# Eight modulation sums, four low parts and the order at the turn in a one-core decoder layer

## The chip, the cores and the metric

The kernel runs on one core of a Trainium2 chip. The core has a matrix engine (TensorE, called PE in the profile, with its weight loads as PEld), VectorE (DVE), ScalarE (ACT), GpSimd (POOL) and SyncE (SP), which only issues transfers; ACT and POOL issue transfers as well. Each engine runs its own list of instructions in order and waits for the others by semaphores. The metric is device time in microseconds (us), the median over several executions; less is better. The profile is of one further execution.

## The reference

One decoder layer over 512 positions of 1024 channels, in float32. A condition vector `c` gives six modulation vectors of 1024 numbers each, and the layer is a mixer followed by a gated convolution block:

```python
cond = jax.nn.silu(c)
mod = cond @ ada_w[l] + ada_b[l]
sh1, sc1, g1, sh2, sc2, g2 = jnp.split(mod[:, None, :], N_MOD, axis=-1)
...                                   # mixer: mLSTM heads and a convolution group
x = x + g1 * rms_norm(mix, mix_post_g[l])
u = rms_norm(x, ffn_pre_g[l]) * (1.0 + sc2) + sh2
up = causal_dwconv(u @ ffn_up[l], ffn_conv_w[l], ffn_conv_b[l])   # 3 taps
a, gt = jnp.split(up, 2, axis=-1)
f = (jax.nn.silu(gt) * a) @ ffn_down[l]                           # 2816 -> 1024
x = x + g2 * rms_norm(f, ffn_post_g[l])
```

The last modulation vector, `g2`, is used only in the last line, after the down projection.

## The kernel before

**Precision.** Every large product is made of three matmuls: each operand is split into a high part, which ACT rounds into a tile `...h`, and a low part `...l`, the operand minus its high part; high times high, low times high and high times low are added up in PSUM (`mm3`, L188 to L190, and L1093, L1459). So each tile of 128x512 weights costs ACT one instruction and somebody one subtraction. There are two ways for the subtraction. `split` (L1011 to L1015) and `w_split` (L169 to L172) let VectorE or GpSimd subtract. `added_split` (L1081 to L1087) has ACT write the negated operand into the low tile (L1085), and a GpSimd transfer that accumulates (L1086) adds the operand onto its rounded negative.

**Modulation.** The 6144 modulation numbers are 48 columns of 128. Each column is one sum: a 128x1024 row block of the transposed weights is loaded into a tile of the pool `adas` (two buffers of 512 KB each) and VectorE multiplies it with the condition and sums over the row (L155 in `ada_block`, L1149 in `ada_add`; the profile names the output `junk`). Columns 40 to 47 belong to `g2`. After them come `ada_done(40, 48)`, which adds the bias, and `gain(3, ...)`, both small.

**The up projection.** 22 units, each of 256 columns (128 of `a`, 128 of the gate), go in two ways. Units 0 to 7 are plain (`plain_unit`): the loop over m = 0 to 3 takes two units a turn, each of 48 matmuls of 128x512 (units 0 to 2 are begun in halves while the mixer ends). Each unit's result stands in two PSUM banks; ACT and VectorE apply the three taps (`conv3`, L995 and L997; `fa5c` is the `a` half of unit 5, `fg5c` its gate half), and `unit_out` (L1140) writes the product into a tile `F`. For i = 3 and 4 `token_forms` makes sums of the inputs on GpSimd (L1059) and VectorE.

Units 8 to 21 go in seven stages, m = 4 to 10. A stage takes one unit by a Strassen-like scheme (products p1, p7, p5, p6 first, L1093, into banks `upx`, `upz`, `upw`; then four VectorE sums in `between`, L1111 to L1114; then p2, p3, p4) and one plain unit, whose two halves stand between and behind. In a stage PE's order is: first products of the even unit, first half of the plain unit, last products of the even unit, second half of the plain unit. The forms of the next unit's weights (L1299, L1314, L1345, L1346, L1361) are VectorE subtractions of loaded blocks, followed by ACT and GpSimd splits. In stages 4 to 7 two modulation columns a stage are fetched and summed (`ada_fetch`, `ada_add`).

**The down projection.** 11 groups of weights, m = 0 to 10, in two passes. In the first pass VectorE makes three sums of the loaded blocks of a group (`forms1`, L1190 to L1192), four operands are split (`b_m` is the plain block, `t_m` the three sums), and PE makes the products p1, p5, p7 and p6, of six matmuls each for two token halves' banks. `part_b` gives the plain block's low part to the accumulating transfer; without it `parts1` has VectorE subtract it. In the kernel before, groups 0 to 5, 8, 9 and 10 have `part_b`. For groups 9 and 10 PE takes p1 of both, p5 of both, p6 of both, p7 of both: the *turn*. There VectorE adds the product sums to each other (`su`, L1439, then L1441, L1445, L1447), and the second pass adds p2, p3 and p4 (L1459) onto the same banks, with its own loads (`load2`), one VectorE sum (L1254) and three splits a group (`forms2`). `b_0` to `b_10` and `t_0` to `t_10` are names of both passes.

**What sets the order.** The lists of PE and SP are as written in the program. VectorE, ACT and GpSimd keep the written order inside three `in_order()` blocks (the end of the mixer with the first up halves; the stages 4 to 10 together with the first pass of the down projection and the turn; the last outputs). Elsewhere, as in the plain units and in the loop of the second pass, a scheduler that simulates the engines orders them by priorities and dependencies. A transfer that ACT issues stands in ACT's list, and the work behind it waits until its buffer is free.

Of the kernel before, what the change touches and what calls it, by code (L numbers as in the profile page):

```python
# [52 lines left out]
def decoder_layer(ctx, tc, w_glu0, x, xT, c, adaT, vecs, w_glu, w_qko, w_v0, w_v, w_out, w_up, w_down, out):  # L53
# [890 lines left out]
    with in_order():  # L944
        for tt in range(3):
            mix_last(tt, 0, 2 * KT - KA)
        up_split(1, raw1, slots, "t")
        r = chain_sums(0)
        up_split(1, raw1, slots, "t")
        r = chain_x(0, r)  # L950
        chain_u(0, r)
        turn_tile(0)
        mix_last(3, 0, 7)
        r = chain_sums(1)
        up_split(1, raw1, slots, "t")
        r = chain_x(1, r)
        chain_u(1, r)
        turn_out(0)
        turn_tile(1)
        mix_last(3, 7, 2 * KT - KA)  # L960
        r = chain_sums(2)
        turn_out(1)
        r = chain_x(2, r)
        up_split(1, raw1, slots, "t")
        chain_u(2, r)
        up_half(0, 0)
        turn_tile(2)
        r = chain_sums(3)
        up_split(2, raw2, wpool, "w")
        r = chain_x(3, r)  # L970
        up_split(2, raw2, wpool, "w")
        chain_u(3, r)
        up_half(0, 1)
        up_split(2, raw2, wpool, "w")
        early.append([cvbank(f"up2_{half}") for half in range(2)])
        up_half(0, 2, 0)
        turn_tile(3)
        turn_out(2)
        up_split(2, raw2, wpool, "w")
        turn_out(3)  # L980
    up_half(0, 2, 1)
# [156 lines left out]
    def unit_out(i, a, g, F):  # L1138
        S.activation(g, g, AF.Silu)
        V.tensor_tensor(out=F[:, (i % 2) * T : (i % 2 + 1) * T], in0=a, in1=g, op=ALU.mult)  # L1140

    def ada_fetch(i):
        r = adas.tile([P, D], F32, tag="ada", name=f"ada_{i}")
        nc.scalar.dma_start(r, adaT[i // 2][:, (i % 2) * D : (i % 2 + 1) * D])
        return r

    def ada_add(i, r):
        junk = small.tile([P, D], BF16, tag="junk", bufs=1, name=f"junk_{i}")
        V.scalar_tensor_tensor(out=junk, in0=r, scalar=1.0, in1=cb, op0=ALU.mult, op1=ALU.mult, accum_out=mod[:, i : i + 1])  # L1149
# [100 lines left out]
    def forms2(m, a=0, b=3):  # L1250

        r = loaded[m]
        if b == 3:
            behind_turn(V.tensor_tensor(out=r[2], in0=r[0], in1=r[2], op=ALU.subtract))  # L1254
        return parts(r, [(f"b2_{m}", 0), (f"b4_{m}", 1), (f"t4_{m}", 2)][a:b])
# [8 lines left out]
    for m in range(MS):  # L1264
        open_F(m)
        for i in (2 * m, 2 * m + 1):
            pa, pg = plain_unit(i)
            if m < MS - 1:
                unit_out(i, conv3(pa, i, f"fa{i}"), conv3(pg, NF + i, f"fg{i}"), Fs[m])
            elif i % 2 == 0:  # L1270
                even = pa, pg
# [18 lines left out]
    with in_order():  # L1290
# [14 lines left out]
        for m in range(MS, NM):  # L1305
# [50 lines left out]
            if more_to_come:  # L1356
# [3 lines left out]
                ada = [(n, ada_fetch(n)) for n in range(40 + 2 * (m - MS), 42 + 2 * (m - MS))] if m < MS + 4 else []  # L1360
# [13 lines left out]
            for n, r in ada:  # L1374
                ada_add(n, r)
            if m == MS + 4:
                ada_done(40, 48)
                gain(3, 40, "ffn_post_g")
# [19 lines left out]
        for m in range(3, NM):  # L1398
            forms1(m)
            if m < 6 or NM - G2A <= m < NM - 1:  # L1400
                part_b(m)
            parts1(m)
            if m == NM - 2:
                part_b(NM - 1)
# [18 lines left out]
        w2 = {}  # L1423
        for which in ("p1", "p5", "p6", "p7"):
            for m in range(M1, NM):
                prod1(m, which)
            if which == "p1":
# [3 lines left out]
                w2[0] = forms2(0)  # L1431
            elif which == "p5":
                sp5 = [slot(f"sp5_{q}") for q in range(2)]
                for q in range(2):
                    S.activation(sp5[q], p5[q], AF.Copy)
            elif which == "p6":
# [5 lines left out]
                w2[1] = forms2(1, 0, 1)  # L1442
            else:
# [4 lines left out]
                w2[1] |= forms2(1, 1, 3)  # L1448
# [17 lines left out]
    for m in range(NM):  # L1466
# [3 lines left out]
        if m > 1:  # L1470
            w2[m] = forms2(m)
# [140 lines left out]
```

## Time and profile before

| | |
|---|---|
| median of 3 runs | 780.53 us (780.48 to 781.32) |
| the profiled execution | 779.45 us |
| its span, first to last instruction | 777.7 us |
| PE busy | 757.8 us, 97% of the span |
| VectorE busy | 643.7 us, 83% |
| ACT busy | 449.3 us, 58% |
| GpSimd busy | 370.6 us, 48% |
| granted TensorE clock, mean | 0.996 |

Times in the trace count from the span's start. 1.75 us of the profiled execution lie outside its span, and it is 1.08 us below the median. The plain units of the up projection end at about 506 us, the stages 4 to 10 run from there to 656 us, the first pass of the down projection to 723 us and the second pass to the end.

A row of the waits view is: who waited, for whom, us in total, times, longest. A row of the windows view gives, for a stretch of time, its length, then PE, PEld, VectorE, ACT and GpSimd busy (with the number of instructions), the granted clock, the transfers' share of the 16 DMA engines, and GB/s. A row of the timeline is start, length, engine, line, operation, out<-in, shape, and in brackets the idle time ahead of it with what ended it.

### The profile page before, as it was taken

How to read it: one execution, taken by the hardware profiler on the slowest of the kernel's cores; microseconds unless marked ns; L12 is line 12 of the kernel's file. 1: busy time of each engine (PE TensorE's matmuls, PEld its weight loads, DVE VectorE, ACT ScalarE, POOL GpSimd, SP SyncE). 2: the span in 40 equal slices, each digit the busy share in tenths (PEclk: the TensorE clock that was granted, in tenths of full speed). 3: DMA queues.
4: the chain of work that ended last, by engine and by line, in shares of the span. 5: the costliest groups of instructions: out<-in, count | busy, mean ns of one | idle time of the engine just before them, and what ended most of it. 6: DMA issues, size and time to landing. Idle time of an engine off the chain costs nothing.

```text
span 777.7 us, 11564 instructions
## 1 busy us (share of the span) xinstructions
PE 757.8 (97%) x3961; PEld 645.3 (83%) x3961; DVE 643.7 (83%) x1030; ACT 449.3 (58%) x864; POOL 370.6 (48%) x324
## 2 busy tenths in 40 slices
PE   7999999999999999999999999999999999998996
PEld 6888898778888888988889988898889898876774
DVE  6978999999999856737868489779999868985986
ACT  5547276776676365761345466666675766655652
POOL 2039587796796743442841355455555652100001
PEclk9999999999999999999999999999999999999999
DMA  9973214123031551437853488798888899799682
GB/s 330 388 276 133 83 58 176 65 83 109 28 136 54 189 191 55 163 108 255 314 197 128 136 209 235 205 243 222 235 215 208 198 229 251 209 373 360 239 296 108
DMA packets 56575, 149.52 MB, mean 192 GB/s; under 512 B 6434, under 2 KB 7874, under 8 KB 52420
## 3 DMA queue, kind: packets, MB, share of 16 engines
q1 hardware_dynamic: 33588, 100.37, 37.3%
q10 hardware_dynamic: 14288, 32.68, 12.2%
q0 software_dynamic: 8640, 15.73, 11.4%
q8 instruction: 31, 0.51, 0.3%
q14 instruction: 28, 0.23, 0.1%
HBM read 117.42 MB, written 15.61 MB: 171 GB/s over the span
## 4 chain that ended last, share of the span: by engine, by line
PE 55%; DVE 29%; DMA 8%; issue 3%; ACT 3%; ACTq 1%; SPq 0%; POOL 0%; DVEq 0%; POOLq 0%
DVE cv L731 10%; PE up L189 5%; PE up L188 5%; PE up L190 5%; PE glu L316 3%; PE glu L190 3%; PE glu L189 3%; PE glu L188 3%; PE upx L1093 2%; DVE junk L1149 2%; PE mixa L188 2%; PE mixa L190 2%; PE mixa L189 2%; PE mixb L188 2%; PE mixb L189 2%
## 5 line engine op out<-in xcount | busy, mean ns | idle before, releaser
L731 DVE SCALAR_TENSOR_TENSOR cv<-gt,cvw,cv 128x505 f32<-128x505 f32 (+24 forms) x200 | 137.2, 728 | 2.3 <-ACT cv L719 1.1
L727 POOL TENSOR_TENSOR cs<-cs,cs 128x510 f32<-128x510 f32 (+3 forms) x32 | 42.0, 1313 | 0.3
L725 ACT ACTIVATE cs<-gt,cvw 128x511 f32<-128x511 f32 (+4 forms) x40 | 27.4, 717 | 6.8 <-POOL cs L727 3.5
L685 POOL TENSOR_TENSOR ro2r<-ro2t,mhalf 128x1 f32<-128x1 f32 x1 | 0.6, 561 | 55.9 <-DVE ro2t L683 55.9
L189 PE MATMUL up<-u2l,wup_0h 128*128 128x512 f32 (+1 forms) x72 | 25.7, 356 | 0.2 <-DVE u2l L910 0.2
L188 PE MATMUL up<-u2h,wup_0h 128*128 128x512 f32 (+1 forms) x72 | 25.6, 356 | 0.0
L190 PE MATMUL up<-u2h,wup_0l 128*128 128x512 f32 (+1 forms) x72 | 25.4, 353 | 0.0
L171 POOL TENSOR_TENSOR wglu_0l<-wglu,wglu_0h 128x512 fp32r<-128x512 f32 x4 | 5.8, 1455 | 40.5 <-ACT wglu_0h L170 40.5
L171 POOL TENSOR_TENSOR wqko_1024l<-wqko,wqko_1024h 128x512 fp32r<-128x512 f32 x12 | 16.3, 1360 | 18.4 <-ACT wqko_1024h L170 13.0
L155 DVE SCALAR_TENSOR_TENSOR junk<-ada,cb 128x1024 bf16<-128x1024 f32 x12 | 19.8, 1651 | 4.4 <-DMA ada<-in_adaT 4.1
L155 DVE SCALAR_TENSOR_TENSOR junk<-spare,cb 128x1024 bf16<-128x1024 f32 x12 | 18.0, 1504 | 4.0 <-DMA spare<-in_adaT 3.7
L188 PE MATMUL qko<-uh,wqko_1024h 128*128 128x512 f32 x48 | 20.6, 430 | 0.0
L188 PE MATMUL qko<-uh,wqko_0h 128*128 128x512 f32 x48 | 20.2, 420 | 0.0
L276 DVE SCALAR_TENSOR_TENSOR junk<-ada,cb 128x1024 bf16<-128x1024 f32 x16 | 19.5, 1218 | 0.1
L171 POOL TENSOR_TENSOR wo_512l<-wo,wo_512h 128x512 fp32r<-128x512 f32 x8 | 12.9, 1617 | 13.8 <-ACT wo_512h L170 13.8
L171 POOL TENSOR_TENSOR wqko_0l<-wqko,wqko_0h 128x512 fp32r<-128x512 f32 x12 | 16.6, 1385 | 5.0 <-ACT wqko_0h L170 5.0
L190 PE MATMUL qko<-uh,wqko_1024l 128*128 128x512 f32 x48 | 18.8, 392 | 0.0
L190 PE MATMUL qko<-uh,wqko_0l 128*128 128x512 f32 x48 | 18.8, 391 | 0.0
L171 POOL TENSOR_TENSOR wqko_512l<-wqko,wqko_512h 128x512 fp32r<-128x512 f32 x12 | 17.0, 1417 | 3.6 <-ACT wqko_512h L170 3.6
L189 PE MATMUL qko<-ul,wqko_1024h 128*128 128x512 f32 x48 | 18.7, 390 | 0.0
L189 PE MATMUL qko<-ul,wqko_0h 128*128 128x512 f32 x48 | 18.7, 390 | 0.0
L190 PE MATMUL qko<-uh,wqko_512l 128*128 128x512 f32 x48 | 18.7, 389 | 0.0
(1247 smaller groups left out, 3129.1 us busy)
## 6 DMA issues: line engine op xcount, KB each, us to landing
wups<-in_w_up SPq DMA_DIRECT2D x56, 256.0 KB, 5.2
wqko<-in_w_qko SPq DMA_DIRECT2D x12, 1024.0 KB, 4.7
ada<-in_adaT ACTq DMA_DIRECT2D x20, 512.0 KB, 4.7
ada<-in_adaT SPq DMA_DIRECT2D x16, 512.0 KB, 6.6
wo<-in_w_out SPq DMA_DIRECT2D x8, 1024.0 KB, 4.8
wup<-in_w_up SPq DMA_DIRECT2D x8, 1024.0 KB, 7.0
spare<-in_adaT ACTq DMA_DIRECT2D x12, 512.0 KB, 7.2
wd<-in_w_down SPq DMA_DIRECT2D x20, 256.0 KB, 6.7
```

The lines of the kernel that those rows point to most:

```text
L155: t = V.scalar_tensor_tensor(out=junk, in0=r, scalar=1.0, in1=cb, op0=ALU.mult, op1=ALU.mult, accum_out=mod[:, i : i + 1])
L171: (eng or G).tensor_tensor(out=lo[:, :n], in0=src, in1=hi[:, :n].bitcast(F32), op=ALU.subtract)
L188: PE.matmul(ps, a[0], b[0], start=start, stop=False)
L189: PE.matmul(ps, a[0], b[1], start=False, stop=False)
L190: PE.matmul(ps, a[1], b[0], start=False, stop=stop)
L276: V.scalar_tensor_tensor(out=junk, in0=first[k][:, i * D : (i + 1) * D], scalar=1.0, in1=cb, op0=ALU.mult, op1=ALU.mult, accum_out=part[k] ...
L316: PE.matmul(banks0[i], blk(wk, i)[a], u[k][b], start=k == 0 and a == b, stop=False)
L725: S.activation(t[:, d:], cvx[j][:, : T - d], AF.Copy, scale=w(CK - 1 - d))
L727: G.tensor_tensor(out=side[:, d:], in0=side[:, d:], in1=t[:, d:], op=ALU.add)
L731: last_tap[0] = V.scalar_tensor_tensor(out=cp[:, d:], in0=cvx[j][:, : T - d], scalar=w(CK - 1 - d), in1=cp[:, d:], op0=ALU.mult, op1=ALU.add)
L1093: PE.matmul(ps, x, y, start=start and k == 0 and n == 0, stop=stop and k == NT - 1 and n == 2, skip_group_check=True)
L1149: V.scalar_tensor_tensor(out=junk, in0=r, scalar=1.0, in1=cb, op0=ALU.mult, op1=ALU.mult, accum_out=mod[:, i : i + 1])
```

## The change

Three things.

1. The columns 40 to 47 of the modulation leave the stages 4 to 7. Columns 40 to 43 are summed after the mixer's tokens have been turned, as early as their loads and VectorE allow; columns 44 to 47 behind the output products of units 4 and 5. `ada_done` and `gain` follow unit 5. `ada_fetch` and `ada_add` go.
2. In the down projection's first pass, groups 5, 8, 9 and 10 no longer have `part_b`: their plain block's low part is a VectorE subtraction, as for groups 6 and 7. Group 10's plain block is split with the rest of group 10.
3. At the turn, `forms2(0)` (the sum) and two splits of group 0 come ahead of the turn's products, the third split behind p1; group 1's sum and first split come behind p1 as well, its second behind p5 and its third at the end.

```diff
+    for n in range(40, 44):
+        ada_block(n, last_lo[0])
     up_half(0, 2, 1)
...
-    def forms2(m, a=0, b=3):
-
+    def forms2(m):
         r = loaded[m]
-        if b == 3:
-            behind_turn(V.tensor_tensor(out=r[2], in0=r[0], in1=r[2], op=ALU.subtract))
-        return parts(r, [(f"b2_{m}", 0), (f"b4_{m}", 1), (f"t4_{m}", 2)][a:b])
+        behind_turn(V.tensor_tensor(out=r[2], in0=r[0], in1=r[2], op=ALU.subtract))
+
+    def parts2(m, a=0, b=3):
+        return parts(loaded[m], [(f"b2_{m}", 0), (f"b4_{m}", 1), (f"t4_{m}", 2)][a:b])
...
-                unit_out(i, conv3(pa, i, f"fa{i}"), conv3(pg, NF + i, f"fg{i}"), Fs[m])
+                done = unit_out(i, conv3(pa, i, f"fa{i}"), conv3(pg, NF + i, f"fg{i}"), Fs[m])
+                if i > 3:
+                    for n in (2 * i + 36, 2 * i + 37):
+                        ada_block(n, done)
+                if i == 5:
+                    ada_done(40, 48)
+                    gain(3, 40, "ffn_post_g")
...
-                ada = [(n, ada_fetch(n)) for n in range(40 + 2 * (m - MS), 42 + 2 * (m - MS))] if m < MS + 4 else []
...
-            for n, r in ada:
-                ada_add(n, r)
-            if m == MS + 4:
-                ada_done(40, 48)
-                gain(3, 40, "ffn_post_g")
...
             forms1(m)
-            if m < 6 or NM - G2A <= m < NM - 1:
+            if m < 5:
                 part_b(m)
             parts1(m)
-            if m == NM - 2:
-                part_b(NM - 1)
...
         w2 = {}
+        forms2(0)
+        w2[0] = parts2(0, 0, 2)
         for which in ("p1", "p5", "p6", "p7"):
             for m in range(M1, NM):
                 prod1(m, which)
             if which == "p1":
...
-                w2[0] = forms2(0)
+                w2[0] |= parts2(0, 2, 3)
+                forms2(1)
+                w2[1] = parts2(1, 0, 1)
             elif which == "p5":
...
+                w2[1] |= parts2(1, 1, 2)
             elif which == "p6":
...
-                w2[1] = forms2(1, 0, 1)
             else:
...
-                w2[1] |= forms2(1, 1, 3)
+                w2[1] |= parts2(1, 2, 3)
```

PE's and SP's lists keep their order. The other engines' lists change at three places that matter. Lines of the changed kernel stand one to eleven lines away from those of before (L1014 is L1016, L1299 is L1298, L1254 is L1245).

The first place is VectorE between the product of unit 5 (`F<-fa5c,fg5c`) and the sum L1299 that the first stage's p6 waits for. Before, from one row ahead of that product on:

```order
L997 SCALAR_TENSOR_TENSOR fg5c<-up_1_4886,vec,fg5c 128x510
L1140 TENSOR_TENSOR F_4728<-fa5c,fg5c 128x512
L1022 TENSOR_TENSOR ysum<-F_4728 128x256
L1023 TENSOR_TENSOR F_4728<-F_4728 128x256
L1024 TENSOR_TENSOR ysum<-ysum,F_4728 128x256
L1025 TENSOR_TENSOR ysq<-F_4728,ysum 128x256
L997 SCALAR_TENSOR_TENSOR fa6c<-up_0_4962,vec,fa6c 128x511
L1036 TENSOR_TENSOR fl_0_4926<-F_4728,fh_0_4925 128x512
L997 SCALAR_TENSOR_TENSOR fa6c<-up_0_4962,vec,fa6c 128x510
L1299 TENSOR_TENSOR wups_5084<-wups_5084 128x512
```

And in the changed kernel:

```order
L999 SCALAR_TENSOR_TENSOR fg5c<-up_1_4910,vec,fg5c 128x510
L1142 TENSOR_TENSOR F_4744<-fa5c,fg5c 128x512
L155 SCALAR_TENSOR_TENSOR junk_4947,mod<-ada_4945,cb 128x1024
L1024 TENSOR_TENSOR ysum<-F_4744 128x256
L999 SCALAR_TENSOR_TENSOR fa6c<-up_0_4996,vec,fa6c 128x511
L155 SCALAR_TENSOR_TENSOR junk_4951,mod<-ada_4949,cb 128x1024
L1025 TENSOR_TENSOR F_4744<-F_4744 128x256
L1026 TENSOR_TENSOR ysum<-ysum,F_4744 128x256
L999 SCALAR_TENSOR_TENSOR fa6c<-up_0_4996,vec,fa6c 128x510
L1298 TENSOR_TENSOR wups_5118<-wups_5118 128x512
```

Two of the eight sums now stand ahead of that weight sum, and two more, of columns 44 and 45, stand behind the product of unit 4, further ahead in the same list. `ysq` and `fl` have gone behind it.

The second place is ACT at the plain block of group 10. Before:

```order
L1013 ACTIVATE t_9h<-wdmore 128x512 x3
L1084 ACTIVATE b_10h<-wdmore 128x512
L1085 ACTIVATE b_10l<-wdmore 128x512
L1013 ACTIVATE g2h_7383<-g2kept 128x512
L1013 ACTIVATE s_7385<-g2kept 128x256
L1013 ACTIVATE t_10h<-wdmore 128x512 x3
```

Changed:

```order
L1015 ACTIVATE t_9h<-wdmore 128x512 x3
L1015 ACTIVATE g2h_7375<-g2kept 128x512
L1015 ACTIVATE s_7377<-g2kept 128x256
L1015 ACTIVATE b_10h<-wdmore 128x512
L1015 ACTIVATE t_10h<-wdmore 128x512 x3
```

`g2h` no longer stands behind a block that comes with group 10's load, and the negated copy is gone; on VectorE the subtraction of `b_10l` stands directly ahead of the three of `t_10l`.

The third place is VectorE at the turn. Before, from the last split of group 0 on:

```order
L1014 TENSOR_TENSOR t_0l<-wd_11_7316,t_0h 128x512
L1439 TENSOR_TENSOR su_7473<-p_0_6910,sp_0_7428 128x512
L1439 TENSOR_TENSOR su_7474<-p_1_6911,sp_1_7429 128x512
L1441 TENSOR_TENSOR p_0_6908<-p_0_6908,su_7473 128x512
L1441 TENSOR_TENSOR p_1_6909<-p_1_6909,su_7474 128x512
L1014 TENSOR_TENSOR b_1l<-wd_12_7378,b_1h 128x512
L1445 TENSOR_TENSOR p_0_6912<-p_0_6912,su_7473 128x512
L1445 TENSOR_TENSOR p_1_6913<-p_1_6913,su_7474 128x512
L1447 TENSOR_TENSOR sp_0_7457<-p_0_6912,sp_0_7457 128x512
L1447 TENSOR_TENSOR sp_1_7458<-p_1_6913,sp_1_7458 128x512
L1254 TENSOR_TENSOR wd_12_7378<-wd_12_7378 128x512
L1014 TENSOR_TENSOR b_1l<-wd_12_7378,b_1h 128x512
```

Changed:

```order
L1016 TENSOR_TENSOR t_0l<-wd_11_7314,t_0h 128x512
L1245 TENSOR_TENSOR wd_12_7370<-wd_12_7370 128x512
L1016 TENSOR_TENSOR b_1l<-wd_12_7370,b_1h 128x512 x2
L1435 TENSOR_TENSOR su_7478<-p_0_6910,sp_0_7433 128x512
L1435 TENSOR_TENSOR su_7479<-p_1_6911,sp_1_7434 128x512
L1437 TENSOR_TENSOR p_0_6908<-p_0_6908,su_7478 128x512
L1437 TENSOR_TENSOR p_1_6909<-p_1_6909,su_7479 128x512
L1440 TENSOR_TENSOR p_0_6912<-p_0_6912,su_7478 128x512
L1440 TENSOR_TENSOR p_1_6913<-p_1_6913,su_7479 128x512
L1442 TENSOR_TENSOR sp_0_7458<-p_0_6912,sp_0_7458 128x512
L1442 TENSOR_TENSOR sp_1_7459<-p_1_6913,sp_1_7459 128x512
L1016 TENSOR_TENSOR t_1l<-wd_12_7370,t_1h 128x512
```

Group 1's sum (on `wd_12`, its loaded tile) and both its `b` splits now stand ahead of `su`, and the eight adds of the turn follow each other without a split between.

More of the change, by code (lines that the diff above doesn't have):

```diff
@@ L1139, in unit_out @@
         S.activation(g, g, AF.Silu)
[L1140 to L1149, printed above, removed]
+        return V.tensor_tensor(out=F[:, (i % 2) * T : (i % 2 + 1) * T], in0=a, in1=g, op=ALU.mult)
     def own_out(m):
@@ L1470, in decoder_layer @@
         if m > 1:
-            w2[m] = forms2(m)
+            forms2(m)
+            w2[m] = parts2(m)
         if M2 - NT <= m < M2:
```

## The prediction

> **What bounds the kernel now.** I read the page's busy times first, then PE's waits, the clock and the stretches stage by stage, and last the single waits on the timeline.
>
> ```profile
> PE 757.8 (97%) x3961; PEld 645.3 (83%) x3961; DVE 643.7 (83%) x1030; ACT 449.3 (58%) x864; POOL 370.6 (48%) x324
> ```
>
> PE is busy for 757.8 of 777.7 us, so an edit that removes no product can gain only where PE waits, or where its own steps are slow. The waits near the change, and the stretches (length; PE, PEld, VectorE, ACT, GpSimd; clock, DMA share, GB/s):
>
> ```profile
> PE p L189 <- DMA b_10l<-wdmore: 2.6, 1, 2.6
> PE p L189 <- DMA b_5l<-wdmore: 1.7, 1, 1.7
> PE upx L1093 <- ACT fh L1030: 1.7, 2, 0.9
> PE p L1459 <- DVE t_10l L1014: 0.8, 1, 0.8
> PE p L1459 <- DVE t_9l L1014: 0.5, 1, 0.5
> ...
> 562.96:585.04 22.08, 21.23 (x134) 19.00 (x134) 20.14 (x29) 14.29 (x26) 12.27 (x11) 1.00 0.89 221
> 607.10:628.20 21.10, 21.10 (x136) 19.08 (x134) 16.01 (x28) 14.29 (x26) 11.44 (x11) 1.00 0.83 199
> ...
> 677.00:723.00 46.00, 41.64 (x176) 33.63 (x175) 35.53 (x59) 23.49 (x45) 3.51 (x4) 0.96 1.03 359
> 713.40:716.60 3.20, 3.20 (x9) 2.50 (x9) 1.59 (x3) 2.22 (x5) 0.00 (x0) 0.52 1.05 408
> ```
>
> The row of 22.08 us is a stage with two modulation sums, the row of 21.10 one without: there PE never stops, VectorE has 4.1 us less to do, and the stage is a microsecond shorter. The change's first part acts here. The stretch 677 to 723 holds the other loss: 4.4 us without PE work, a mean clock of 0.96 with 3.2 us at 0.52, and DMA engines full throughout.
>
> **The sums leave the stages.** Of each stage, the first of its last products on PE:
>
> ```profile
> 517.18 0.28 PE L1093 MATMUL upx<-u2h,wup_p2h 128*128 128x256 f32 x1
> ...
> 604.74 0.36 PE L1093 MATMUL upx<-u2h,wup_p2h 128*128 128x256 f32 x1 [0.86 <-ACT fh L1030]
> ...
> 646.92 0.28 PE L1093 MATMUL upx<-u2h,wup_p2h 128*128 128x256 f32 x1
> ```
>
> Four stages with sums take 604.74 - 517.18 = 87.56, two without 646.92 - 604.74 = 42.18, or 21.09 each. Four such are 84.36: a gain of **3.2**. I see no other reason for the difference, since PE's work is the same.
>
> **Where they go.** The price of one sum in the stages, and VectorE's idle time in the two new places:
>
> ```profile
> L1149 DVE SCALAR_TENSOR_TENSOR junk<-ada,cb x8: 1217/2146/3091, 527.5 to 595.1; 128x1024 bf16<-128x1024 f32 x8
> ...
> 433.00:447.00 14.00, 14.00 (x119) 14.00 (x119) 5.45 (x9) 5.83 (x9) 2.77 (x3) 1.00 0.53 151
> ...
> DVE wups L1294 <- POOL wup_p1l L171: 1.3, 1, 1.3
> DVE fg6c L997 <- ACT fg6c L995: 1.2, 1, 1.2
> ```
>
> The smallest, 1.22, is a sum alone; the median is 2.15, and the largest, 3.09, is one beside GpSimd work. Columns 40 to 43 come to about 433 to 447, where VectorE is busy for 5.45 of 14.00 and GpSimd for 2.77. Four at 1.22 and 0.4 of small pieces are 5.3, into 8.55 of idle time: they cost nothing. At 3.09 each they are 12.8 and VectorE leaves this stretch 4.2 late, with PE's plain products, which run without a stop, still ahead of it. If no idle time covered them, they would cost PE up to 5.3.
>
> Columns 44 to 47 stand ahead of the weight sum L1299, on which the first stage's p6 hangs; queued behind them are that sum and the four of `between` (L1111 to L1114), for which PE waits ahead of its last products. They add 4 x 1.22 + 0.4 = 5.3. Of idle time they can use 2.5 (the rows of 1.3 and 1.2 above; the remaining waits are round trips to ACT that stay). The slack is
>
> ```profile
> 494.17 1.29 POOL L171 TENSOR_TENSOR wup_p5l<-wups,wup_p5h 128x512 fp32r<-128x512 f32 x1
> 499.57 0.68 DVE L1299 TENSOR_TENSOR wups<-wups 128x512 f32<-128x512 f32 x1
> 513.26 0.42 DVE L1113 TENSOR_TENSOR upx<-upx,u 128x256 f32<-128x256 f32 x1
> ```
>
> 3.5 us: L1113 is done at 513.7 and its reader starts at 517.18. Alone, then, the sums make VectorE 2.8 late, and PE waits for nothing. If two of them meet a GpSimd split and lose its 1.29, VectorE is 5.4 late and PE waits 1.9. All four at 3.09 make it 10.3 late and PE waits 6.8. GpSimd splits in short pieces here, not in long ones as in the stages, so I take **1.5**, nearer the lower end. This part is 3.2 - 1.5 = **1.7**, with ends 3.2 and -3.6.
>
> What GpSimd can do to VectorE stands in this pair:
>
> ```profile
> 473.13 5.76 DVE L1025 TENSOR_TENSOR ysq<-F,ysum 128x256 f32<-128x256 f32 x1
> 473.25 5.35 POOL L1059 TENSOR_TENSOR b<-u2h,u2l 128x512 f32<-128x512 f32 x4
> ```
>
> A 256-wide VectorE sum took 5.76 beside 5.35 of GpSimd, though a 512-wide one takes 0.68 above. If all four sums lose a whole split of 1.29, VectorE is 5.3 + 5.2 - 2.5 = 8.0 late, PE waits 4.5, and this part comes to -1.3. That is what a rule of the Trainium skill would have ("SBUF — State Buffer", section "Who interferes with whom"): a VectorE instruction with two SBUF inputs and a GpSimd one that reads SBUF contend, and the second to issue is blocked for the whole of it. By that rule, the trace agrees at `ysq`; it decides nothing on how often the two meet.
>
> **Low parts in the down projection.** The two waits that the change takes on, and the rows around them:
>
> ```profile
> 678.96 1.90 DVE L1014 TENSOR_TENSOR t_5l<-wdmore,t_5h 128x512 fp32r<-128x512 f32 x3
> 686.02 0.50 PE L189 MATMUL p<-b_5l,fh 128*128 128x512 f32 x1 [1.73 <-DMA b_5l<-wdmore]
> 687.36 0.69 DVE L1014 TENSOR_TENSOR b_6l<-wdmore,b_6h 128x512 fp32r<-128x512 f32 x1 [1.66 <-ACT b_6h L1013]
> ...
> 703.47 0.63 ACT L1084 ACTIVATE b_10h<-wdmore 128x512 fp32r<-128x512 f32 x1 [1.13 <-DMA wdmore<-in_w_down]
> 705.02 0.87 POOL L1086 DMA_DIRECT2D b_10l<-wdmore  x1 [4.46 <-ACT b_10l L1085]
> 705.17 0.69 DVE L1014 TENSOR_TENSOR g2l<-g2kept,g2h 128x512 fp32r<-128x512 f32 x1 [1.95 <-ACT g2h L1013]
> 708.28 1.89 DVE L1014 TENSOR_TENSOR t_10l<-wdmore,t_10h 128x512 fp32r<-128x512 f32 x3
> 709.92 0.45 SPq L1240 DMA_DIRECT2D wd<-t2d  x1
> 712.11 0.50 PE L189 MATMUL p<-b_10l,fh_0b 128*128 128x512 f32 x1 [2.63 <-DMA b_10l<-wdmore]
> 712.22 0.69 DVE L1254 TENSOR_TENSOR wd<-wd 128x512 f32<-128x512 f32 x1 [1.11 <-DMA wd<-t2d]
> ```
>
> A VectorE subtraction is 0.69, or 0.63 in a run of three.
>
> *b_5l.* Put ahead of `t_5l`, it is ready about 679.6, against 684.29 (686.02 - 1.73) when PE wants it. Gain **1.7**. Its 0.63 is taken up by the 1.66 of idle time at 687.36.
>
> *b_10l.* PE wants `b_10l` at 709.48 (712.11 - 2.63), and with the 1.7 above at 707.75. VectorE: `t_10l` began at 708.28; the 1.95 waited for `g2h` goes, since ACT no longer stops for `b_10h` ahead of it; the subtractions for groups 8 and 9 add 1.2; so it gets there at 707.55 and has `b_10l` done at 708.2. Wait 0.5 in place of 2.63: gain **2.1**, with ends 0 (group 10's load lands no sooner, and ACT splits `b_10h` late) and 2.63.
>
> *The clock.* The row at 0.52 begins 0.4 us after the 2.63 us gap; the gap of 1.73 was followed by none. Gone with the gap, it returns half of 3.2: **1.6**.
>
> *Transfers.* Four accumulating transfers less:
>
> ```profile
> q0 software_dynamic: 8640, 15.73, 11.4%
> ```
>
> 60 of 256 KB take 11.4% of 777.7, 1.48 each of all 16 engines; four are 5.9 of a stretch whose share was 1.03. They also leave GpSimd, which has nothing queued behind them. I book no gain of its own: PE no longer waits for a load there once both low parts are VectorE's. This covers the faster start of the second pass, whose loads would otherwise bind.
>
> **The turn.** `t_10l` ends at 710.1, as before; `g2l` and its half-width partner at 711.2; then come seven of 0.69 at most (group 0's sum and three splits, group 1's sum and two), to 716.0. Group 0's load, which stood at 709.92 in SP's list behind PE and was used 2.3 later, comes with PE by about 710.5. `su` needs p6, which PE now has 5.4 earlier than 719.95:
>
> ```profile
> 719.95 1.37 DVE L1439 TENSOR_TENSOR su<-p,sp 128x512 f32<-128x512 f32 x2 [3.05 <-PE p L190]
> 723.15 0.39 PE L1459 MATMUL p<-b_0h,g2h 128*128 128x512 f32 x1
> 725.43 0.68 DVE L1254 TENSOR_TENSOR wd<-wd 128x512 f32<-128x512 f32 x1
> 730.84 0.68 DVE L1014 TENSOR_TENSOR b_2l<-wdmore,b_2h 128x512 fp32r<-128x512 f32 x1
> 731.31 0.39 PE L1459 MATMUL p<-b_2h,g2h 128*128 128x512 f32 x1
> 740.37 0.39 PE L1459 MATMUL p<-b_4h,g2h 128*128 128x512 f32 x1
> ```
>
> PE begins the second pass 5.4 (1.7 + 2.1 + 1.6) earlier than 723.15, at 717.75. A group there takes 4.08 (723.15 to 731.31 is two), so its second product, which needs the adds to p5, comes at 719.1 and its third, which needs those to p7, at 720.5. With `su` at 716.0 and 1.3 for each pair the adds end at 718.7 and 719.9: in time, though with 0.4 to spare. Group 2's sums and first split end near 724.3, and PE wants `b_2` at 725.9. Before, `b_2l` was done at 731.52, 0.2 after PE's start on that group, so PE ran behind it: groups 0 and 1 took 8.16, groups 2 and 3 took 9.06. I book **0.6** of that 0.9. The waits for `t_9l` and `t_10l` (1.3) stay, as their work is unchanged.
>
> **Sum.** 3.2 - 1.5 + 1.7 + 2.1 + 1.6 + 0.6 = 7.7 us. The profiled execution is 779.45, the span 777.7 and 1.75 around it; it falls to 771.75. The median lies 1.08 above the profiled execution, so I say **772.8**.
>
> **Rivals.**
> *The opening debt.* VectorE reaches L1299 late by 6.7 or more, so that the gap in the first stage takes all of the 3.2 or more, while the down projection gains its 6.0: from 780.53 - 6.0 = 774.5 to 778.1, and 775.8 with four blocked splits. For it speaks the `ysq` pair, against it that splits there are pieces of 1.29 and not a row of four.
>
> *The loads bind the turn.* DMA engines were at 1.03 of a full share, and group 1's `wd` must land ahead of its sum, which now stands before `su`; if it lands at 717 or later (the row of 725.43 gives no earlier bound), `su` is late, and with it p5, p7 and groups 2 to 4. Then the down projection gives only some 3 and the median is about 775.9. Against it: 5.9 of transfers go.
>
> *The half clock stays.* It follows some other gap, for instance of the two waits at the end of the first pass: 772.8 + 1.6 = 774.4. The Trainium skill, "TensorE: Matmul & The Clock Gate", section "What's actually happening", tells of a throttle that follows an idle window of about 3.4 us; the trace's gap of 2.63 was followed by 0.52 and that of 1.73 was not, so the rows set the bound lower.
>
> *Nothing moves in the down projection.* Group 10's load sets the end of the first pass, the freed engines make no difference: only 1.7 remains, 778.8.
>
> *Slower.* One mechanism: all four sums run beside GpSimd at 3.09, and none of the 2.5 of idle time can take them, since the waits for splits grow with them. VectorE is 12.8 late at L1299, PE waits 9.3 in the first stage, and after a gap that long its clock is halved for 3.2 us as at 713.4, 1.6 more: 10.9 against 9.2 of other gains (3.2 and 6.0), or 782.2. It decides from 11.1 of lateness on (3.5 + 9.2 - 1.6) and needs every sum at the top of the prices.
>
> **Chances.** Forecast 0.55, with its own range 770.5 (no opening wait, and all of the 2.63) to 774.5; opening debt 0.16; loads 0.15; half clock 0.05; nothing in the down projection 0.05; slower 0.04. Range **769.2 to 777.8**: below, 770.5 less the 1.3 that I count as staying; above, past the middle of the opening debt and the loads. What a measurement here can tell from no change is 0.2%, 1.6 us: faster means below 779. Faster **0.91**, the same **0.05**, slower **0.04**: the same holds half of the case in which the down projection gives nothing, and mixtures of it with a debt.
>
> **What will show it.** Stages 5 to 7 should take 21.1 each, with no wait at `upx`; the first stage should show one gap ahead of its last products, 0 to 2 us, and the four sums ahead of L1298 at 1.2 to 2.5 each. There should be no wait for `b_5l`, one of under 1 us for `b_10l`, by VectorE and not a transfer, and a clock of 1.00 from 677 on. The second pass should begin 7 us earlier than 723.15, 1.7 of them from the stages. I am wrong if sums of 3 us stand ahead of L1298 and PE stops there for over 4 us, if `su` comes after a load, or if the gap at group 10 remains.

## The result

The changed kernel takes 772.31 us in the median of 5 runs (770.89 to 774.77), where the kernel before took 780.48 beside it. The ratio is 0.9901 (95% interval 0.9875 to 0.9928): 1.0% faster. The forecast was 772.8. Run again on another occasion it took 771.65, ratio 0.9893 (0.9862 to 0.9923). The profiled execution is 770.89, against 779.45 before: 8.56 us less, where the forecast's sum was 7.7.

The profile after, busy times and PE's waits from 500 us on:

```profile
PE 754.2 (98%) x3961; PEld 644.7 (84%) x3961; DVE 641.4 (83%) x1034; ACT 449.0 (58%) x860; POOL 367.6 (48%) x320
...
PE p L189 <- DMA b_0l<-wd: 1.4, 1, 1.4
PE upx L1095 <- DVE upx L1115: 1.1, 1, 1.1
PE p L1454 <- DVE t_10l L1016: 0.4, 1, 0.4
PE up L188 <- DVE fa7c L999: 0.2, 1, 0.2
```

The waits for `b_5l`, `b_10l` and `t_9l` are gone, as are those at `upx` in the stages 6 to 8. What stands there now is the forecast wait in the first stage, and one that the prediction didn't have: 1.4 us at `b_0l`, the low part of the down projection's first group. Windows of a stage that had the sums, and of the stretch with the half clock (length; PE, PEld, VectorE, ACT, GpSimd; clock, DMA share, GB/s):

```profile
539.98:561.06 21.08, 21.08 (x134) 19.12 (x134) 16.71 (x26) 14.59 (x26) 12.27 (x12) 1.00 0.84 205
677.00:716.00 39.00, 39.00 (x173) 32.28 (x172) 37.62 (x64) 23.68 (x45) 0.00 (x0) 1.00 1.02 373
```

The stage takes 21.08, as the stages without sums did before, and from 677 to the second pass PE doesn't stop and its clock is 1.00 throughout. The DMA engines are as full as before (1.02).

PE's list is the same in both kernels, so the same matmul can be found in both traces. These are the markers in the changed kernel, on PE's timeline:

```profile
518.92 0.36 PE L1095 MATMUL upx<-u2h,wup_p2h 128*128 128x256 f32 x1 [1.12 <-DVE upx L1115]
603.26 0.28 PE L1095 MATMUL upx<-u2h,wup_p2h 128*128 128x256 f32 x1
656.95 0.50 PE L189 MATMUL p<-b_0l,fh 128*128 128x512 f32 x1 [1.41 <-DMA b_0l<-wd]
657.29 0.40 PE L190 MATMUL p<-b_0h,fl 128*128 128x512 f32 x1
707.63 0.39 PE L190 MATMUL p<-b_10h,fl_0b 128*128 128x512 f32 x1
716.70 0.39 PE L1454 MATMUL p<-b_0h,g2h 128*128 128x512 f32 x1
733.02 0.39 PE L1454 MATMUL p<-b_4h,g2h 128*128 128x512 f32 x1
```

For every profiled run I took the starts of the same matmuls: the first product of stage 4 (505.96 before), the first of its last products (517.18), that of stage 8 (604.74), the third matmul of group 0 (657.16), of group 5 (686.36), of group 10 (712.45), the second pass's first (723.15), its group 4 (740.37), and the last matmul of all (770.61). Each stretch between two of them holds one term of the prediction. The table gives the length of each stretch less its length in the kernel before, in us; minus is a gain.

| profiled run | up to stage 4 | opening | stages | b_0l | b_5l | b_10l | clock | turn | end | behind stage 4's start, in all |
|---|---|---|---|---|---|---|---|---|---|---|
| forecast | 0 | +1.5 | -3.2 | 0 | -1.7 | -2.1 | -1.6 | -0.6 | 0 | -7.7 |
| changed kernel | 0.0 | +1.75 | -3.21 | +1.61 | -1.98 | -2.97 | -1.64 | -0.89 | -1.23 | -8.56 |
| the same again | -0.4 | +2.42 | -3.48 | +1.11 | -1.98 | -2.97 | -1.64 | -0.89 | -1.42 | -8.85 |
| sums alone | +2.0 | +1.69 | -3.48 | -0.08 | +0.25 | -0.26 | -0.07 | 0.00 | -0.67 | -2.62 |
| low parts alone | -0.1 | 0.00 | +1.18 | 0.00 | -2.00 | -2.92 | -1.58 | +0.01 | +0.65 | -4.66 |
| turn alone | +2.1 | 0.00 | +0.16 | +0.02 | -0.61 | +0.16 | -0.02 | -0.89 | -0.71 | -1.89 |
| short sums in the stages | +2.4 | 0.00 | -3.56 | +0.71 | -0.29 | +0.12 | -0.13 | 0.00 | -0.73 | -3.88 |
| b_10l by transfer | +0.3 | +1.22 | -3.49 | +0.98 | -1.94 | -0.62 | -1.62 | -0.89 | -0.47 | -6.83 |
| group 1 late | -0.2 | +1.23 | -3.04 | +1.60 | -1.98 | -2.97 | -1.64 | 0.00 | -0.09 | -6.89 |
| b_0l by VectorE | +0.7 | +2.44 | -3.21 | -0.08 | -2.00 | -2.72 | -1.62 | -0.87 | -1.17 | -9.23 |
| one sum a stage | -0.5 | 0.00 | -3.56 | +0.30 | -1.98 | -2.97 | -1.64 | -0.89 | -1.07 | -11.81 |
| both | +2.6 | 0.00 | -3.56 | -0.08 | -2.00 | -2.69 | -1.62 | -0.14 | -0.44 | -10.53 |

The first column moves by up to 3 us between executions. From the matmul at 430.6 on, ahead of all sums that were moved, PE takes 75.34 us to stage 4 in every one of these profiles, so what moves it lies in work that no kernel here changes. So single profiles are compared from stage 4's start on, in the last column, and whole times by their medians.

### The profile page after: what moved, and what is told of

It reads as the page before. It is cut to its first block, busy times and chain, and to the rows that moved or that the text cites. A ratio compares the mean times of both kernels' runs of the same rounds, so it can differ in the third digit from the quotient of the medians.

```text
span 769.2 us, 11554 instructions
## 1 busy us (share of the span) xinstructions
PE 754.2 (98%) x3961; PEld 644.7 (84%) x3961; DVE 641.4 (83%) x1034; ACT 449.0 (58%) x860; POOL 367.6 (48%) x320
## 4 chain that ended last, share of the span: by engine, by line
PE 59%; DVE 27%; DMA 5%; ACT 4%; issue 3%; ACTq 1%; POOL 0%; DVEq 0%; SPq 0%; POOLq 0%
DVE cv L731 10%; PE up L189 4%; PE up L190 4%; PE up L188 4%; PE upx L1095 4%; PE glu L316 3%; PE glu L189 3%; PE glu L190 3%; PE glu L188 3%; PE p L189 3%; PE p L190 3%; PE p L188 3%; PE mixa L188 2%; PE mixa L190 2%; PE mixa L189 2%
## 5 line engine op out<-in xcount | busy, mean ns | idle before, releaser
L155 DVE SCALAR_TENSOR_TENSOR junk<-ada,cb 128x1024 bf16<-128x1024 f32 x20 | 31.2, 1562 | 7.9 <-DMA ada<-in_adaT 7.7
L276 DVE SCALAR_TENSOR_TENSOR junk<-ada,cb 128x1024 bf16<-128x1024 f32 x16 | 19.5, 1219 | 0.1
```

What stands on the lines that cost most here:

```text
L155: t = V.scalar_tensor_tensor(out=junk, in0=r, scalar=1.0, in1=cb, op0=ALU.mult, op1=ALU.mult, accum_out=mod[:, i : i + 1])
L276: V.scalar_tensor_tensor(out=junk, in0=first[k][:, i * D : (i + 1) * D], scalar=1.0, in1=cb, op0=ALU.mult, op1=ALU.mult, accum_out=part[k] ...
```

## The experiments

**The three parts alone.** Each kernel is the one before with one of the three parts of the change.

*Sums alone*: columns 40 to 47 leave the stages, nothing else.

```diff
+    for n in range(40, 44):
+        ada_block(n, last_lo[0])
...
+                if i > 3:
+                    for n in (2 * i + 36, 2 * i + 37):
+                        ada_block(n, done)
...
-                ada = [(n, ada_fetch(n)) for n in range(40 + 2 * (m - MS), 42 + 2 * (m - MS))] if m < MS + 4 else []
```

> Only the eight sums move; low parts and the turn stay as before. By the prediction's sum this alone is worth 1.7 us: 778.8. By what the changed kernel's trace suggests (the stages gain 3.4 after 1.7 of loss at the opening, but the first group's low part, a transfer, lands no sooner, and PE waits about 1.4 for it; the transfer for b_5l lands no sooner either), only 0.2 to 0.5 us is left: about 780.2, with waits of PE at b_0l near 1.4 and at b_5l near 1.9.

Measured: 778.94 us, ratio 0.9974 (0.9957 to 0.9992). By the interval it gains 0.6 to 3.4 us: the prediction's 1.7 is in it, and my reading after the result, 0.2 to 0.5, is not. The profile has +1.69 at the opening and -3.48 in the stages, which is 1.8. But there is no wait at `b_0l` in this execution, so PE's lead wasn't lost there, and I had been wrong to expect that it always is.

*Low parts alone*: groups 5, 8, 9 and 10.

```diff
-            if m < 6 or NM - G2A <= m < NM - 1:
+            if m < 5:
                 part_b(m)
             parts1(m)
-            if m == NM - 2:
-                part_b(NM - 1)
```

> Only the low parts of groups 5, 8, 9 and 10 go to VectorE; sums and turn as before. Prediction: 1.7 + 2.1 + 1.6 = 5.4 us, 775.1. If the wait for b_10l goes altogether, as in the changed kernel, 6.3 us by the end of the first pass; if the old order at the turn then makes PE wait for su, group 1's parts or the second pass's loads, 1 to 2 of it come back: 774.2 to 776.2. No 0.52 clock behind 713 in either case.

Measured: 774.35 us, ratio 0.9919 (0.9892 to 0.9947). The three stretches of the first pass gain 2.00, 2.92 and 1.58, the same as in the changed kernel, so they need neither of the other parts. The turn gains nothing, and the end loses 0.65. The +1.18 in the stages has no edit behind it: those stages are as before, and in this execution PE waited 3.0 us for `fh` there and not 1.7. Why was not looked into; in these stages PE waits by 0.7 to 1.3 us each time, so one wait more makes the difference.

*The turn alone*: group 0's and group 1's forms ahead.

```diff
+        forms2(0)
+        w2[0] = parts2(0, 0, 2)
...
-                w2[0] = forms2(0)
+                w2[0] |= parts2(0, 2, 3)
+                forms2(1)
+                w2[1] = parts2(1, 0, 1)
```

> Only the order at the turn changes. Prediction: 0.6 us, 779.9, with the waits for t_9l and t_10l at the end unchanged (0.5 and 0.8). Rival: the split t_1l comes about 2.6 us earlier against PE's second pass, and the loads of later groups, which stand behind it in SP's list, with it: then the waits for t_9l and t_10l shrink as well, 0.9 + 1.4 = 2.3 us, 778.2. The wait for b_10l (2.6) and the clock of 0.52 behind it stay.

Measured: 778.79 us, ratio 0.9968 (0.9942 to 0.9994), 2.5 us by the ratio. The turn gains 0.89, the end 0.71 more with no wait left at `t_9l`: the rival's way, though `t_10l` still waits 0.8. But the end is 0.67 better and without a wait at `t_9l` in the sums alone too, whose turn is as before, so this run by itself doesn't show that the end's gain comes from the turn. The wait at `b_10l` and the half clock stay.

The parts' ratios add up to 1.4%, with intervals of 0.2 to 0.3% each, against 1.0 to 1.1% for the whole.

**What made the stages longer.** The kernel before, with each of the eight sums in the stages taken over 8 columns of 1024; their transfers stay.

```diff
-        V.scalar_tensor_tensor(out=junk, in0=r, scalar=1.0, in1=cb, op0=ALU.mult, op1=ALU.mult, accum_out=mod[:, i : i + 1])
+        V.scalar_tensor_tensor(out=junk[:, :8], in0=r[:, :8], scalar=1.0, in1=cb[:, :8], op0=ALU.mult, op1=ALU.mult, accum_out=mod[:, i : i + 1])
```

> The kernel before, but each of the eight sums in the stages goes over 8 of its 1024 columns; all transfers and their issues on ACT stay (so the modulation vector g2 is not computed). If VectorE's time is what makes stages 4 to 7 longer, they take 21.1 us each instead of 21.9, without waits at upx. If it is ACT, held at the issue of the two loads, or the loads' traffic, they stay at 21.9. In the first case PE reaches the down projection 3.2 us earlier and loses 2 to 3 of that again at b_0l and b_5l: 779 to 780.

Measured: 777.79 us, ratio 0.9984 (0.9956 to 1.0013). The whole time doesn't tell it from no change; the stages do. One of them:

```profile
541.00:562.10 21.10, 21.10 (x135) 19.18 (x134) 16.62 (x30) 14.62 (x27) 12.16 (x11) 1.00 0.99 250
```

It takes 21.10, PE never stops, and the stretch gains 3.56, though ACT still issues both loads. So the sums' time on VectorE was the cause, not the loads. Here the gain was spent in part: 0.71 at `b_0l`, where PE waits as in the changed kernel.

**The low part of group 10 and the half clock.** The changed kernel, with that low part given back to the transfer.

```diff
             parts1(m)
+            if m == NM - 2:
+                part_b(NM - 1)
```

> The changed kernel with group 10's low part given back to the accumulating transfer, split ahead of the rest of the group as before. If the prediction's two terms for b_10l and the clock are right, PE waits 2 to 2.7 us at b_10l and runs at about half clock for 3.4 us behind that: 4.2 to 4.6 us more than the changed kernel, 776.5 to 777. If the half clock of before had another cause than this gap, 2.5 to 3 us more. If the three transfers fewer in this stretch let it land in time, no wait and no half clock: less than 1 us more.

Measured: 775.44 us, ratio 0.9932 (0.9906 to 0.9959). The wait is back, and 2.35 of the 2.97, but the half clock is not. In form that is the second of the outcomes that I had written, but not for its reason, that the half clock has another cause than the gap. Beside it the same place in the kernel with the sums alone, each with the matmul behind the gap and two windows:

```profile
708.54 0.50 PE L189 MATMUL p<-b_10l,fh_0b 128*128 128x512 f32 x1 [2.08 <-DMA b_10l<-wdmore]
...
704.26:707.67 3.41, 2.20 (x10) 1.50 (x8) 3.38 (x7) 3.30 (x7) 0.00 (x0) 1.00 1.07 317
707.67:711.08 3.41, 2.54 (x11) 2.13 (x12) 1.65 (x3) 1.68 (x4) 0.00 (x0) 1.00 1.04 396
```

```profile
712.21 0.60 PE L189 MATMUL p<-b_10l,fh_0b 128*128 128x512 f32 x1 [2.24 <-DMA b_10l<-wdmore]
...
709.05:712.46 3.41, 1.17 (x6) 0.67 (x5) 2.29 (x5) 1.01 (x3) 0.00 (x0) 1.00 1.08 324
712.46:715.88 3.42, 3.42 (x9) 2.63 (x9) 0.59 (x2) 1.92 (x4) 0.00 (x0) 0.50 1.05 410
```

Over all profiles of the down projection gaps of 2.24, 2.63, 2.64 and 2.77 were followed by 3.41 us in which a matmul took 0.43 in place of 0.23, and gaps of 2.08 and less were not. Length alone need not be what divides them, for the granted clock changes on a grid. In the kernel before it falls to half at 713.08, is full again from 716.49 and falls once more at 774.51, 18 steps of 3.41 later, and in each of the twelve profiles all its changes lie on one such grid of its own. The windows above are steps of these grids. The gap of 2.24 lies in one step, and in that step PE is busy for 1.17 of 3.41. With the transfer, the next change of the clock is at 769.11, so a line lies 18 steps ahead of it, at 707.67: the gap of 2.08 lies across that line, and neither of its steps has less than 2.20 of work. Of all steps at full clock in the twelve profiles, those with 2.13 us or more without PE work were followed by half clock, and those with up to 1.86 were not (group 1 late, 762.58 to 765.99, and one sum a stage, 757.19 to 760.60, with 1.28 and 1.55 busy). So by these rows it isn't enough that the gap is there: more than half of one step must fall into it, and where the grid lies differs from execution to execution. No run moved a gap or changed its length alone. The Trainium skill, "TensorE: Matmul & The Clock Gate", section "What's actually happening", puts the slow clock behind an idle window of about 3.4 us, in windows that run freely. The grid of 3.41 us agrees with that; the steps that brought the slow clock on still held up to 1.28 us of PE work, and the measurement decides.

**What carries the turn.** The changed kernel, with group 1's sum and splits at their old places.

```diff
-                forms2(1)
-                w2[1] = parts2(1, 0, 1)
             elif which == "p5":
...
-                w2[1] |= parts2(1, 1, 2)
             elif which == "p6":
...
+                w2[1] = parts2(1, 0, 1)
             else:
...
-                w2[1] |= parts2(1, 2, 3)
+                forms2(1)
+                w2[1] |= parts2(1, 1, 3)
```

> The changed kernel with group 1's sum and splits at the places they had before the change; group 0 stays early. If t_1l, behind which SP's later loads stand, carries the second pass, the waits at b_2 (0.9 in all) and of 0.7 at t_9l come back: 1.5 to 2.0 us more than the changed kernel, 773.8 to 774.3. If group 0's early start carries it, as the prediction's words on the turn have it, less than 0.4 us more.

Measured: 773.31 us, ratio 0.9906 (0.987 to 0.9941). The medians are 1.0 apart, inside their spread. The profile is plain: the turn's gain is 0.00 in place of 0.89, and the end's 0.09 in place of 1.23. `t_1l` in the kernel before and in the changed one, each with SP's first load behind it:

```profile
727.83 0.68 DVE L1014 TENSOR_TENSOR t_1l<-wd,t_1h 128x512 fp32r<-128x512 f32 x1
...
728.54 0.33 SPq L1238 DMA_DIRECT2D wd<-in_w_down  x1
```

```profile
718.70 0.68 DVE L1016 TENSOR_TENSOR t_1l<-wd,t_1h 128x512 fp32r<-128x512 f32 x1
...
719.41 0.33 SPq L1231 DMA_DIRECT2D wd<-in_w_down  x1
```

In both the load starts 0.71 us behind the start of the split, when its buffer is free; the transfer before it in SP's list was issued at 719.49 before and at 714.19 after, so SP's list had stood still for nine us and now for five. Against PE's second pass (723.15 and 716.70) the split comes at +4.68 before and at +2.00 after. In all five profiles with the old order of group 1 it is at +4.68 or +4.69, groups 2 and 3 take 9.1 and the turn gains nothing; in the six with the new order and the split at +2.00 to +2.19 the turn gains 0.87 to 0.89. Two things hang on that split. The splits of groups 2 and 3 stand behind it in VectorE's own list: that is the turn's 0.89. And the later loads stand behind its buffer in SP's: VectorE's last sum, ahead of `t_9l`, waits for one of them, before and in the changed kernel:

```profile
756.85 0.69 DVE L1254 TENSOR_TENSOR wdmore<-wdmore 128x512 f32<-128x512 f32 x1 [0.82 <-DMA wdmore<-t2d]
```

```profile
748.28 0.69 DVE L1245 TENSOR_TENSOR wdmore<-wdmore 128x512 f32<-128x512 f32 x1 [1.42 <-DMA wdmore<-t2d]
```

Against the second pass's start that is +33.7 and +31.6: the load lands 2.1 sooner. Over the profiles that sum starts at +33.0 to +34.4 with the split at +4.68 and at +31.4 to +32.4 with the split at +2.00 to +2.19. So group 1's place carries the turn, and not group 0's; and it carries a part of the end's gain, whose size is not settled. With the split at +4.68 PE waits at `t_9l` in three profiles (0.45, 0.38, 1.14) and not in the sums alone and the short sums, and the end moves from 0.65 lost to 0.73 gained; with it at +2.00 to +2.19 the end gains 0.47 to 1.42. By the end alone the two orders overlap; turn and end together keep them apart, with 0.7 gained at most under the old one and 1.4 to 2.3 under the new.

**The wait that came new.** The changed kernel, with group 0's low part subtracted by VectorE.

```diff
             else:
-                part_b(0)
                 part_b(1)
```

> The changed kernel with group 0's low part subtracted by VectorE too. If the wait of 1.4 us at b_0l in the changed kernel is that transfer among the loads that now start 0.7 us behind it, it goes, VectorE has 0.6 us for it in a stage with 5 us of idle time, and PE keeps 1.4 to 1.7 us to the end: 770.6 to 771.0. Rival: the gain is given back at b_10l, where VectorE comes just in time: 0.7 us at most is kept, 771.6 or more.

Measured: 770.25 us, ratio 0.9866 (0.9837 to 0.9895), a little better than the range written, though this interval and that of the changed kernel touch. The wait goes, and nothing later takes it back: b_5l, b_10l, clock, turn and end keep their gains. Its own issue, and the first of the next group's loads on SP, in the changed kernel and in the kernel before:

```profile
648.87 0.87 POOL L1088 DMA_DIRECT2D b_0l<-wd  x1 [4.75 <-PE upx L1095]
...
649.61 0.33 SPq L1173 DMA_DIRECT2D wd<-in_w_down  x1
```

```profile
650.04 0.87 POOL L1086 DMA_DIRECT2D b_0l<-wd  x1 [4.37 <-PE upx L1093]
...
652.19 0.33 SPq L1180 DMA_DIRECT2D wd<-in_w_down  x1
```

Before, the loads came 2.15 us behind the transfer and it landed after 5.2; now they come 0.74 behind and it lands after 8.0. In turn alone, low parts alone, sums alone, short sums and one sum a stage: 2.9 behind and 5.7, 1.9 and 4.9, 1.2 and 6.6, 0.6 and 7.1, 0.6 and 6.8. PE wants it 6.4 to 7.5 us after the issue. Wherever the loads come 0.6 to 0.7 behind, PE waits: 0.8 to 1.4 us in four profiles of the changed kernel and its variants, 0.5 in short sums, 0.1 in one sum a stage; where they come 1.2 behind or later, it doesn't wait. What SP's list stands for ahead of these loads is the landing of `wup_3l`, the last low part of the up projection. SP's waits there, before and in the changed kernel:

```profile
SPq L1180 <- DMA wup_3l<-wups: 3.4, 1, 3.4
```

```profile
SPq L1173 <- DMA wup_3l<-wups: 2.3, 1, 2.3
```

It lands at 652.1 before and at 649.5 now, 2.6 earlier, and `b_0l` is issued only 1.2 earlier: so the loads move up to it. That transfers of different engines end on the same 16 DMA engines and interleave there is also what the Trainium skill says, "DMA: Bandwidth & Descriptors", section "Issuing engines are not separate DMA queues"; the landing times agree. That the near loads cause the late landing was not tested by moving them.

**The opening.** The changed kernel, with columns 44 to 47 one in each of the stages 4 to 7.

```diff
-                if i > 3:
-                    for n in (2 * i + 36, 2 * i + 37):
-                        ada_block(n, done)
...
+                ada = [(n, ada_fetch(n)) for n in range(44 + m - MS, 45 + m - MS)] if m < MS + 4 else []
...
             unit_out(i, vx, vz, Fs[m])
+            for n, r in ada:
+                ada_add(n, r)
```

> The changed kernel with columns 44 to 47 not ahead of the first stage but one in each of the stages 4 to 7. If PE waits in a stage only for what VectorE has above its slack (two sums, 4.1 us, cost 1.09, so the slack is 3), one sum of 1.2 to 3.1 costs nothing there, and the 1.8 us at the opening come back: PE is 3.6 us ahead of the kernel before at the end of stage 7 in place of 1.8; at b_0l it then may wait longer for the transfer, so 770.5 to 772.3 in all. If every sum costs its half, 0.5 us a stage, nothing is gained: 772.3.

Measured: 768.78 us, ratio 0.9847 (0.9818 to 0.9875), better than the whole range written, since the wait at `b_0l` didn't grow with PE's lead (+0.30 in this execution). The opening is back to 0.00 and the stages still gain 3.56. One of these stages, and its four sums (least, median, most, in ns):

```profile
541.00:562.10 21.10, 21.10 (x136) 19.18 (x135) 16.77 (x27) 14.73 (x27) 12.22 (x12) 1.00 0.87 217
...
L1151 DVE SCALAR_TENSOR_TENSOR junk<-ada,cb x4: 1219/1220/1220, 526.0 to 588.6; 128x1024 bf16<-128x1024 f32 x4
```

One sum a stage costs PE nothing, two in each of four stages cost 3.2 to 3.6: what a threshold would give, and not half the price. Alone in its stage each sum also takes 1.22. Of the eight of before the first of each stage took 1.22 and the second 3.1, beside a GpSimd split, so one a stage leaves out more than half of VectorE's time for them, and the runs don't part the number of sums from their meeting GpSimd.

**Both.** The last two edits together.

> Both of the last two edits together: group 0's low part by VectorE, and columns 44 to 47 one in each of the stages 4 to 7. If the two are independent, the stretch behind the mixer gives the 11.8 us of the second of them and the 0.4 us that it still waited at b_0l: 768.2 to 768.6 in all, with no wait of PE over 0.3 us between 500 and the end but that for t_10l. If VectorE, with one sum and one subtraction more, comes late in a stage or at b_5l to b_10l, it is 769 or more.

Measured: 768.57 us, ratio 0.9853 (0.9821 to 0.9884), against 771.65 for the changed kernel beside it on the same chip. That is no better than one sum a stage by what can be told here, and by the medians both beat the two kernels of the case. The median lies in the range written, but the profiled execution, the slowest of the six at 771.56, doesn't show what was expected of it: PE waited 0.4 at `b_3l`, the turn kept only 0.14 of the 0.89, and `t_10l` waited 0.8. `t_1l` comes at +2.90 there. Why was not looked into, and the further gain is not settled. The repeated changed kernel was:

> The changed kernel once more, beside the other on the same chip. If the wait at b_0l belongs to it and is not an accident of one execution, it shows again with 0.8 us or more, behind a landing of 7 us or more of that transfer; if it was an accident, it is missing. Median 771.5 to 772.8.

Measured: 771.65 us, with the wait at `b_0l` at 0.9: it belongs to the kernel.

## Why the prediction was right

The time was right (772.31 for 772.8), and by the table all six of its terms had the right sign and place. But two effects that it didn't have, of opposite sign, nearly cancel: +1.61 and -1.23. That the time came out 0.5 from the forecast is luck in that part.

**The stages** (3.2): 3.21 measured, and short sums shows that VectorE's time is the reason.

**The opening** (1.5 lost): 1.75, 2.42, 1.69, 1.22, 1.23 and 2.44 in the six profiles with those sums. In the changed kernel:

```profile
490.82 2.59 DVE L155 SCALAR_TENSOR_TENSOR junk<-ada,cb 128x1024 bf16<-128x1024 f32 x1
...
499.43 1.22 DVE L155 SCALAR_TENSOR_TENSOR junk<-ada,cb 128x1024 bf16<-128x1024 f32 x1
...
518.35 0.42 DVE L1115 TENSOR_TENSOR upx<-upx,u 128x256 f32<-128x256 f32 x1
```

One of the four met a GpSimd piece and took 2.59; the others took 1.22. L1115 is done at 518.8 where it had been done at 513.7, so VectorE is 5.1 late, against the 5.4 of the middle case. The size is right, but the way to it only in part. In the profile with `b_10l` by transfer all four sums took 1.2, which is the case for which the prediction had VectorE 2.8 late and no wait; there VectorE is 4.6 late against stage 4's start and PE loses 1.22. Beside the sums, the product of unit 5 took 1.54 there and a split `fl` 1.78, both beside GpSimd splits, for 0.90 and 0.68 before, and less than the 2.5 of idle time was used. In the six profiles PE waits 1.06 to 1.12 at `upx`; the two with 2.4 have a second wait, of 0.9 for `fa7c`. That the first four would cost nothing held: PE takes the same 75.34 us from 430.6 to stage 4 with them and without. The pair at `ysq`, from which the price of meeting GpSimd came, shows that the two meet and what it costs VectorE. It doesn't show that the second to issue is the one held up, as the prediction reads it: VectorE's row starts 0.12 us ahead of GpSimd's there, and VectorE's is the one drawn out.

**b_5l** (1.7): 1.98; with the wait goes the slow step behind it, 0.34 in place of 0.23. **The clock** (1.6): 1.64. The half clock began 0.97 us behind the gap's end (713.08 against 712.11), not 0.4 as the prediction has it. The size was right; the prediction set the gap of 2.63 against that of 1.73 by length alone, where by the rows above it is how much of one step of the grid a gap fills.

**b_10l** (2.1): 2.97. Mis-sized. The chain that I added up on VectorE began at its old wait for `g2h` and so left out what VectorE had won before that point:

```profile
699.88 1.89 DVE L1016 TENSOR_TENSOR t_9l<-wdmore,t_9h 128x512 fp32r<-128x512 f32 x3
...
704.67 0.68 DVE L1016 TENSOR_TENSOR b_10l<-wdmore,b_10h 128x512 fp32r<-128x512 f32 x1
```

It starts `b_10l` at 704.67 and not at 707.55. At `t_9l` it was already at 699.88 for 701.32, with 1.2 more work behind it: I had counted the idle 1.66 at 687.36 only as room for the new subtraction, though the whole of it went. VectorE is done 2 us ahead of PE, so no wait is left, and the 0.34 behind it goes too.

**The turn** (0.6): 0.89, the whole of what I had seen there, and as said: PE had run just behind VectorE's splits. The weight loads of groups 2 and 3 in the kernel before show it:

```profile
733.12 0.19 PEld L1459 LDWEIGHTS p<-b_2l,s 128*128 128x128 f32 x1 [0.31 <-DVE b_2l L1014]
734.66 0.19 PEld L1459 LDWEIGHTS p<-t_2l,g2h 128*128 128x128 f32 x1 [0.32 <-DVE t_2l L1014]
```

Five of the new low parts came just late, by 0.3 us each, and the two groups took 0.90 longer for it, in steps too short for PE's own list of waits. What the prediction didn't know is that all of it goes or stays with group 1's place.

**"The waits for `t_9l` and `t_10l` stay, as their work is unchanged"**: this step failed. The wait for `t_9l` is gone and that for `t_10l` is 0.35 for 0.84. Their work is unchanged, but not the time of their loads, which stand in SP's list behind the buffer that `t_1l` frees. How much of the end's 1.23 comes from that is open, since the end moves by up to 0.7 either way without any change at the turn. The prediction asked that of a moved step's own transfers and didn't ask it of the transfers that wait for its buffer.

**`b_0l`**: the other failure, one of omission. The sum carried the stages' gain of 1.7 unchanged to group 5. Between them lay a transfer whose landing doesn't come earlier with PE: `b_0l` was issued 1.2 earlier and landed 1.7 later. So the second pass began 6.45 us earlier and not the 7 of the forecast, though `b_10l` gave 0.9 more than its term. Of the rivals the loads at the turn came nearest in kind, though at another group; none of the rivals took place.

## What to carry to other kernels

A gain upstream is worth only what the next transfer lets through. Follow it to each transfer that PE needs after it, ask how much earlier that one lands, and which loads come to start close behind it. When a step moves, look not only at what it issues but at which buffer it frees and what stands in a queue for that. And work that must be fitted in is best spread below the slack of each place: one sum a stage was free, two in each of four cost 3.2 to 3.6 us, four in one place 1.2 to 2.4.

## What the runs showed of the hardware

The granted clock changes on a grid of 3.41 us here, whose place differs from execution to execution. A step with 2.13 us or more without PE work was followed by half clock and one with up to 1.86 was not; behind the gaps of 2.24 to 2.77 it lasted one step. By this a gap of one length can bring half clock or not, as it falls; that was not tested. And steps far ahead of any edit move by more than the change's smaller terms. In the profiles that start stage 4 two us late, two rows stand in the mixer's opening where the profile of before has one, of 0.5; from the sums alone:

```profile
PE glu L189 <- DVE ul L367: 1.0, 1, 1.0
PE glu L316 <- ACT uh L341: 1.0, 1, 1.0
```

The kernel of that stretch is the same in all runs, and why it falls one way or the other was not looked into. It may be a part of the spread of the times, 777.46 to 782.15 for this one kernel; the executions behind the other times have no profile.
